# Log-sum-exp over 16,384 rows: the first load split into two 64-partition transfers on two queues

## The chip, the cores and the metric

The kernel runs on one core of a Trainium2 chip. The metric is device time in microseconds (us); three runs of the kernel before gave 161.6, 161.67 and 161.76, median 161.67.

The core has engines that run side by side and meet only at semaphores. ScalarE (ACT in the profile) computes exponentials and logarithms, VectorE (DVE) sums, GpSimd (POOL) adds, TensorE (PE) is used here for small checks alone, and SyncE (SP) issues transfers. Sixteen DMA engines move the data between the device's main memory and the on-chip memory, which has 128 partitions (rows).

## The reference

The input `x` is 32 x 512 x 1024 floats: 16,384 rows of 1,024, 67.1 MB. For each row the logarithm of the sum of exponentials is computed:

```python
max_x = np.max(x, axis=-1, keepdims=True)
return (max_x.squeeze(-1) + np.log(np.sum(np.exp(x - max_x), axis=-1))).astype(np.float32)
```

The output is 32 x 512 floats, 65.5 KB.

## The kernel before

**Work and tiles.** Each of the 128 partitions takes 128 rows. The kernel skips the maximum: it takes exponentials as they are, sums them, takes the logarithm, and checks on the side that no sum was too large or too small. Only if that check failed would a second, slower pass with the maximum run (lines 312 to 364); with this input it doesn't.

**The loads.** `LOADS` lists 18 loads by their size in rows per partition: 16, 16, 16, 16, 13.5, 12.5, 9, 7 and so on down to 0.47. A load is one transfer over all 128 partitions, issued on SP's queue by `load` (line 139); a load of 16 rows moves 16,384 floats, 64 KB, into each partition, 8.39 MB in all. Each load has a semaphore `landed[i]` that reaches 16 when all its data is there.

**The ring.** The loads go into `ring`, which has room for 48 rows per partition. Loads 0, 1 and 2 fill it. Load 3 takes the place of load 0 and must wait until the last reader of load 0 has finished; `users` keeps who that is, and `load` makes SP wait for it. So SP's queue is in order: a load that waits for its slots holds up those after it.

**The work on a load.** ACT waits for `landed[i]` and takes exponentials in place (line 228). Then the rows are summed in one of these ways, written behind each load's size in `LOADS`: R, one reduction on DVE (line 239); F, GpSimd adds the two halves of each row (line 233) and DVE reduces what is left (line 171); T, DVE adds the halves and sums in one instruction for each row (line 249); Y and Z, for the last row, ACT sums as it goes (line 202). Loads 0, 1 and 2 are all of kind R. At the end come two logarithms (lines 268, 281), two stores (lines 276, 285) and the check (lines 290 to 308).

**The first load.** A program opens with a barrier in which every engine drains its own queue and then waits for the others (line 407 in the profile, once more at line 62). ACT's first instruction behind it is the load of its function table (line 125). `start_early` takes the instruction of load 0 out of its place when the program is finished and puts it ahead of SP's first drain, so that load 0 is issued before that barrier. Loads 1 and 2 are issued by SP behind the barrier.

## Time and profile before

The profile is of one execution. Its times are in us from its first instruction; `ring<-in_x_dram` means that the ring is written from the input. The engines' busy shares and instruction counts:

| | busy us | share of the span | instructions |
|---|---|---|---|
| DVE | 114.3 | 71% | 59 |
| ACT | 114.5 | 71% | 31 |
| POOL | 37.3 | 23% | 11 |
| PE | 2.2 | 1% | 26 |

| | us |
|---|---|
| median of three runs | 161.67 |
| span of the profiled execution | 160.4 |
| around the span | 1.3 |

Issues of transfers are not counted as busy time; they appear in the timeline under SPq, where q stands for an engine's instruction queue. "mean" or a number of ns is for one instruction. A row in the timeline may merge several instructions (x2, x3): it has the first one's start and the time to the last one's end. In brackets stands how long the engine was idle before, and what ended that.

### The profile page before, as it was taken

The page shows a single profiled execution, that of the slowest core. Times are in us where ns is not written, and L with a number is a line of the kernel's source. Part 1 is how long each engine was busy: PE and PEld are TensorE (multiplying, and loading weights), DVE is VectorE, ACT ScalarE, POOL GpSimd, SP SyncE. Part 2 cuts the span into 40 slices and gives each one's busy share as a digit, 9 for nine tenths or more (in the row PEclk, how much of TensorE's full clock was granted, in tenths as well). Part 3 has the DMA queues.
Part 4 walks back from the last instruction along what each step waited for, and adds up shares of the span by engine and source line. Part 5 has one row for each costly group of instructions (what it writes and reads, how often), then busy time and mean ns, then how long its engine had stood idle before and what let it go on. Part 6 is the DMA issues. An engine that isn't in the chain of part 4 may idle for free.

```text
span 160.4 us, 219 instructions
## 1 busy us (share of the span) xinstructions
PE 2.2 (1%) x26; PEld 1.1 (1%) x26; DVE 114.3 (71%) x59; ACT 114.5 (71%) x31; POOL 37.3 (23%) x11
## 2 busy tenths in 40 slices
PE   0000000000000000000000000000000000000022
PEld 0000000000000000000000000000000000000011
DVE  0000000009999499994999859959999999999996
ACT  3000059990699708995099949991999989799996
POOL 0000000000000000000000994690004969891000
DMA  7996996996996996996999999999999999999992
GB/s 262 523 523 262 523 523 262 523 507 278 523 490 294 523 490 294 523 490 294 482 441 441 441 425 409 409 409 480 432 395 417 450 416 398 448 411 424 412 413 95
DMA packets 2881, 67.18 MB, mean 419 GB/s; under 512 B 576, under 2 KB 704, under 8 KB 1344
## 3 DMA queue, kind: packets, MB, share of 16 engines
q1 hardware_dynamic: 2880, 67.18, 97.7%
q14 instruction: 1, 0.01, 0.0%
HBM read 67.11 MB, written 0.07 MB: 419 GB/s over the span
## 4 chain that ended last, share of the span: by engine, by line
DMA 52%; ACT 28%; DVE 19%; issue 1%; PE 0%
DMA ring<-in_x_dram 52%; ACT ring L228 27%; DVE sumexp L239 15%; DVE sumexp L171 2%; DVE ring L249 1%; DVE over L301 0%; PE count L306 0%; ACT res L268 0%; DVE clamped L290 0%; DVE fine L308 0%; DVE sumexp L212 0%
## 5 line engine op out<-in xcount | busy, mean ns | idle before, releaser
L228 ACT ACTIVATE ring<-ring 128x16384 f32<-128x16384 f32 (+16 forms) x23 | 111.7, 4908 | 43.0 <-DMA ring<-in_x_dram 43.0
L239 DVE TENSOR_REDUCE sumexp<-ring 128x16 f32<-128x16384 f32 (+4 forms) x9 | 85.6, 9513 | 42.7 <-ACT ring L228 42.7
L233 POOL TENSOR_TENSOR ring<-ring 128x3072 f32<-128x3072 f32 (+3 forms) x7 | 37.1, 5313 | 107.3 <-ACT ring L228 107.3
L171 DVE TENSOR_REDUCE sumexp<-ring 128x6 f32<-128x3072 f32 (+3 forms) x7 | 18.4, 2656 | 0.0
L249 DVE SCALAR_TENSOR_TENSOR ring<-ring 128x512 f32<-128x512 f32 x15 | 9.6, 687 | 0.4 <-ACT ring L228 0.4
L125 ACT ACT_TABLE_LOAD x1 | 1.3, 1283 | 1.4 <-PEq L62 1.4
L156 PE MATMUL count<-far,bad 128*1 128x1 f32 x2 | 0.2, 164 | 153.2 <-DVE clamped L151 153.2
L160 PE MATMUL count<-sumexp,ones 128*1 128x1 f32 x18 | 1.6, 164 | 3.6 <-DVE ring L249 3.6
L249 DVE DVE_READ_ACCUMULATOR ring<-ring 128x1 f32 x15 | 1.2, 82 | 0.0
L202 ACT ACTIVATE last_exp<-ring 128x544 f32<-128x544 f32 (+1 forms) x2 | 1.2, 584 | 0.0
L126 DVE MEMSET ones<- 128x1 f32 x1 | 0.1, 59 | 1.5 <-PEq L62 1.5
L156 PEld LDWEIGHTS count<-far,bad 128*1 128x1 f32 x2 | 0.1, 80 | 153.2 <-DVE clamped L151 153.2
L160 PEld LDWEIGHTS count<-sumexp,ones 128*1 128x1 f32 x18 | 0.8, 80 | 4.5 <-DVE ring L249 4.5
L301 DVE SCALAR_TENSOR_TENSOR over<-ring 128x240 f32<-128x240 f32 x1 | 0.4, 404 | 0.0
L308 DVE TENSOR_SCALAR fine<-count 1x1 int32<-1x1 f32 x1 | 0.1, 147 | 0.3 <-PE count L306 0.3
L151 DVE SCALAR_TENSOR_TENSOR clamped<-clamped,sumexp 128x119 f32<-128x119 f32 x1 | 0.3, 283 | 0.0
L268 ACT ACTIVATE res<-sumexp 128x112 f32<-128x112 f32 x1 | 0.3, 279 | 0.0
L281 ACT ACTIVATE res<-last_sum,sumexp 128x1 f32<-128x1 f32 x1 | 0.3, 261 | 0.0
L202 ACT ACTIVATION_READ_ACCUMULATOR last_exp<-ring 128x1 f32 x2 | 0.3, 126 | 0.0
L146 DVE TENSOR_SCALAR clamped<-sumexp 128x119 f32<-128x119 f32 x1 | 0.2, 221 | 0.0
L279 ACT ACTIVATE res<-sumexp 128x15 f32<-128x15 f32 x1 | 0.2, 209 | 0.0
L290 DVE SCALAR_TENSOR_TENSOR clamped<-sumexp 128x9 f32<-128x9 f32 x1 | 0.2, 169 | 0.0
(17 smaller groups left out, 1.8 us busy)
## 6 DMA issues: line engine op xcount, KB each, us to landing
ring<-in_x_dram SPq DMA_DIRECT2D x1, 6912.0 KB, 23.9
ring<-in_x_dram SPq DMA_DIRECT2D x1, 6400.0 KB, 19.7
ring<-in_x_dram SPq DMA_DIRECT2D x1, 4608.0 KB, 15.9
ring<-in_x_dram SPq DMA_DIRECT2D x1, 3584.0 KB, 24.0
ring<-in_x_dram SPq DMA_DIRECT2D x1, 3072.0 KB, 19.1
ring<-in_x_dram SPq DMA_DIRECT2D x1, 2288.0 KB, 24.1
ring<-in_x_dram SPq DMA_DIRECT2D x1, 1664.0 KB, 20.9
ring<-in_x_dram SPq DMA_DIRECT2D x1, 1264.0 KB, 23.6
```

Of the source, the lines that this page charges most:

```text
L125: nc.scalar.preload_act_table_set("natural_log_exp_and_others")
L151: dve.did(nc.vector.scalar_tensor_tensor(out=clamped[:, 0:LATE], in0=clamped[:, 0:LATE], scalar=0.0, in1=sumexp[:, 0:LATE], op0=ALU.bypass ...
L156: pe.did(nc.tensor.matmul(count, lhsT=bad[:, 0:1], rhs=far, start=True, stop=False))
L160: return pe.did(nc.tensor.matmul(count, lhsT=ones, rhs=sumexp[:, c : c + 1], **kw))
L171: at = dve.did(nc.vector.reduce_sum(out=sumexp[:, c0 : c0 + s0], in_=halves, axis=AX.X))
L202: at = act.did(nc.scalar.activation(out=last_exp[:, here - p : end - p], in_=ring[:, here:end], func=AF.Exp, accum_out=first_sum if how == ...
L228: at = act.did(nc.scalar.activation(out=v, in_=v, func=AF.Exp))
L233: at = pool.did(nc.gpsimd.tensor_tensor(out=rows[:, :, 0:H], in0=rows[:, :, 0:H], in1=rows[:, :, H:d], op=ALU.add))
L239: who = (dve, dve.did(nc.vector.reduce_sum(out=sumexp[:, c : c + s], in_=rows, axis=AX.X)))
L249: who = (dve, dve.did(nc.vector.scalar_tensor_tensor(out=lo, in0=lo, scalar=1.0, in1=rows[:, r, H:d], op0=ALU.mult, op1=ALU.add, accum_out ...
L268: ln_early = act.did(nc.scalar.activation(out=res[:, 0:W], in_=sumexp[:, 0:W], func=AF.Ln))
L301: dve.did(nc.vector.scalar_tensor_tensor(out=over[:, 0:half], in0=last_piece[:, 0:half], scalar=CEILING, in1=last_piece[:, half : 2 * half ...
```

## The change

Load 0 is made as two transfers of 64 partitions: partitions 0 to 63 are issued by SP as before, partitions 64 to 127 by ACT, on ACT's own queue. Both add to `landed[0]`, so ACT waits there for 32 instead of 16. `start_early` now moves both instructions, each to a place ahead of the first drain of its own engine. All other loads stay single transfers of 128 partitions on SP's queue.

```diff
-        return nc.sync.dma_start(
-            out=ring[:, here : here + size], in_=source(done_before, size)
-        ).then_inc(landed[i], 16)
+        made = []
+        parts = [(nc.sync, 0, P // 2), (nc.scalar, P // 2, P)] if i == 0 else [(nc.sync, 0, P)]
+        for queue, p0, p1 in parts:
+            made.append(queue.dma_start(
+                out=ring[p0:p1, here : here + size], in_=source(done_before, size)[p0:p1]
+            ).then_inc(landed[i], 16))
+        return made
...
-        first_load = first_load or dma.ins
+        if i == 0:
+            first_loads.extend(one.ins for one in dma)
...
-        act.wait(landed[i], 16)
+        act.wait(landed[i], 16 * len(dma))
...
+        for load in first_loads:
+            here = next(b for b in blocks if any(i.name == load.name for i in b.instructions))
+            k = next(k for k, i in enumerate(here.instructions) if i.name == load.name)
+            assert not here.instructions[k].has_wait()
+            first = here.instructions.pop(k)
+            top = blocks[0].instructions
+            k = next(
+                k for k, i in enumerate(top)
+                if i.engine == first.engine and isinstance(i, mybir.InstDrain)
+            )
+            top.insert(k, first)
```

More of the change, by code (lines that the diff above doesn't have):

```diff
@@ L184 @@
     ln_early = None
-    first_load = None
+    first_loads = []
     for i, (size, ops) in enumerate(loads):
@@ L380, in start_early @@
         blocks = program.main_func.blocks
-        here = next(b for b in blocks if any(i.name == first_load.name for i in b.instructions))
-        k = next(k for k, i in enumerate(here.instructions) if i.name == first_load.name)
-        assert not here.instructions[k].has_wait()
-        first = here.instructions.pop(k)
-        top = blocks[0].instructions
-        k = next(
-            k for k, i in enumerate(top)
-            if i.engine == mybir.EngineType.SP and isinstance(i, mybir.InstDrain)
-        )
-        top.insert(k, first)
+        for load in first_loads:
[9 more added lines that the diff above has]
+            top.insert(k, first)
     nc.at_finalize(start_early)
```

## The prediction

> **What bounds the kernel now.** I read the page first: the sliced view, the queue table and the chain that ended last.

> ```profile
> span 160.4 us, 219 instructions
> ...
> DVE  0000000009999499994999859959999999999996
> ACT  3000059990699708995099949991999989799996
> ...
> DMA  7996996996996996996999999999999999999992
> GB/s 262 523 523 262 523 523 262 523 507 278 523 490 294 523 490 294 523 490 294 482 441 441 441 425 409 409 409 480 432 395 417 450 416 398 448 411 424 412 413 95
> ...
> q1 hardware_dynamic: 2880, 67.18, 97.7%
> ...
> DMA 52%; ACT 28%; DVE 19%; issue 1%; PE 0%
> ```

> The DMA row is full from the first slice to the last but one, and one hardware queue holds the 16 DMA engines for 97.7% of the span, while ACT and DVE have empty slices for the first third. (The 262/523 swing only means that rows of 64 KB are counted when they finish.) Then I asked for busy time by stretch, to see whether the engines have a hole anywhere.

> ```profile
> 0.00:10.00 10.00, 0.00 (x0) 0.00 (x0) 0.15 (x4) 1.28 (x1) 0.20 (x4) 1.00 1.03 419
> 10.00:20.00 10.00, 0.00 (x0) 0.00 (x0) 0.00 (x0) 0.00 (x0) 0.00 (x0) 1.00 0.97 419
> ...
> 60.00:80.00 20.00, 0.00 (x0) 0.00 (x0) 17.87 (x2) 13.86 (x1) 0.00 (x0) 1.00 1.01 437
> 80.00:100.00 20.00, 0.00 (x0) 0.00 (x0) 17.78 (x2) 17.59 (x3) 9.97 (x1) 1.00 1.00 433
> 100.00:120.00 20.00, 0.00 (x0) 0.00 (x0) 18.27 (x5) 16.68 (x4) 6.71 (x1) 1.00 0.95 411
> 120.00:140.00 20.00, 0.00 (x0) 0.00 (x0) 19.70 (x5) 18.43 (x6) 15.75 (x3) 1.00 1.00 431
> ```

> The last two columns are the DMA engines' busy share and GB/s. The only hole is 5% of 20 us, 1 us, between 100 and 120 us. So the transfer stream runs almost unbroken from the first load to the tail, and what lengthens one early load moves all that follows.

> The timeline gives the pace of that stream. A SPq row is the issue of a load; an ACT row in brackets with DMA as its releaser starts when a load has landed.

> ```profile
> 0.00 0.39 SPq L139 DMA_DIRECT2D ring<-in_x_dram  x1
> ```

> ```profile
> 1.45 0.84 SPq L139 DMA_DIRECT2D ring<-in_x_dram  x2
> ```

> ```profile
> 1.45 1.28 ACT L125 ACT_TABLE_LOAD   x1 [1.45 <-PEq L62]
> ...
> 22.00 13.86 ACT L228 ACTIVATE ring<-ring 128x16384 f32<-128x16384 f32 x1 [19.27 <-DMA ring<-in_x_dram]
> 35.89 17.22 DVE L239 TENSOR_REDUCE sumexp<-ring 128x16 f32<-128x16384 f32 x1 [34.23 <-ACT ring L228]
> 41.33 13.86 ACT L228 ACTIVATE ring<-ring 128x16384 f32<-128x16384 f32 x1 [5.46 <-DMA ring<-in_x_dram]
> 55.22 17.22 DVE L239 TENSOR_REDUCE sumexp<-ring 128x16 f32<-128x16384 f32 x1 [2.10 <-ACT ring L228]
> ```

> ```profile
> 60.68 13.86 ACT L228 ACTIVATE ring<-ring 128x16384 f32<-128x16384 f32 x1 [5.49 <-DMA ring<-in_x_dram]
> ...
> 80.02 13.95 ACT L228 ACTIVATE ring<-ring 128x9216 f32<-128x9216 f32 x2 [5.49 <-DMA ring<-in_x_dram]
> ```

> Loads 0 to 3 land at 22.00, 41.33, 60.68 and 80.02 us: 19.33 to 19.35 us for each 128 x 16384 floats, 8.39 MB, or 434 GB/s, 27.1 GB/s for each of 16 engines. That makes load 0's own transfer run from 22.00 - 19.33 = 2.67 us to 22.00 us. With 128 rows over 16 engines, 8 rows each, a row takes 19.33 / 8 = 2.42 us. The smaller loads keep this rate: 433 GB/s between 80 and 100 us with rows of 13.5 and 12.5 thousand floats.

> **The change, part by part.**

> *The issue.* SP's issue of load 0 becomes one for 64 rows, and ACT gains one. Price from the one that starts the timeline: 0.39 us for 128 rows, so 0.2 to 0.39 us on each engine. ACT stands idle at that point, as the rows of the opening barrier show:

> ```profile
> L407 ACTq DRAIN  x1: 8/8/8, 0.1 to 0.1; - x1
> ...
> L407 SPq DRAIN  x1: 133/133/133, 0.4 to 0.4; - x1
> L407 SPq EVENT_SEMAPHORE  x1: 17/17/17, 0.7 to 0.7; - x1
> L407 ACTq EVENT_SEMAPHORE  x1: 17/17/17, 0.7 to 0.7; - x1
> ```

> ACT reaches its drain at 0.1 us and then waits until 0.7. With an issue of up to 0.39 us and a drain that, like SP's, may then take 0.13, it arrives at 0.1 + 0.39 + 0.13 = 0.62 us, against 0.4 + 0.13 = 0.53 for SP now. The barrier moves by 0 to 0.1 us. Behind it on ACT stands the table load (1.45 to 2.73 us), not wanted before 22.00; on SP stand loads 1 and 2, issued at 1.45 and not wanted by the engines before load 0's rows are through at 22 us. The cover is 19 us in both cases, so the cost is nothing. Were the cover gone it would be 0.1 us. The wait of ACT's first exponential on 32 instead of 16 adds no instruction.

> *When the transfer starts.* It begins 2.67 us after its issue by the pace above. Shorter issues could bring that forward: by nothing at the least, by the whole 0.39 us at the most. I take 0, since the 2.28 us that are not issue stay.

> *What the transfer costs as two halves.* This is the term that decides. Each half is 4.19 MB on 64 partitions. If it is spread over all 16 engines, each has 4 rows of SP's half and 4 of ACT's: the same 8 rows, the same bytes. Every load and store of this trace is 128 partitions wide, so no row shows what a 64-partition transfer runs at; I bound it from both sides. Low end: 27.1 GB/s belongs to an engine, whatever partitions it writes. Then 8 rows take 8 x 2.42 = 19.33 us as before: a cost of 0. High end: 27.1 GB/s belongs to a place of entry into the on-chip memory that a fixed set of 8 partitions shares, which with 128 partitions in flight cannot be told from an engine. Sixteen engines that all work on the lower 64 partitions then press through half of the entries, and a row takes 4.84 us. Issued 0.1 us apart, both halves reach every engine in the same order, so the engines take a lower row together, then an upper row together: 8 x 4.84 = 38.7 us, a cost of 19.3 us. Below zero I see no more than the earlier start.

> The trace's nearest rows are the equal paces of loads with 16,384, 13,824 and 12,800 floats a row: a ceiling that doesn't move with the row's length, 16 times one number. A fixed set of 16 ways would give that, and these may sit at the engines or at the on-chip memory. I take the high end, as a judgement: 128 rows in 16 groups of 8 is a layout in which each engine has a way of its own, and 64 rows in 16 groups of 4 is not.

> [...]

> *How far the delay travels.* Load 0 lands at 22.0 + 19.3 = 41.3 us, load 1 behind it at 60.7. Load 3 overwrites load 0's slots and so is issued when DVE's first reduction ends, 35.89 + 17.22 = 53.11:

> ```profile
> 53.14 0.33 SPq L139 DMA_DIRECT2D ring<-in_x_dram  x1
> ```

> It moves to 72.5, while load 2 still occupies the engines to 80.0: the same 7.5 us in hand as now (60.68 - 53.14). Nothing catches up, because ACT and DVE work on a load only after it has landed and every later load sits behind the earlier ones in a stream with 1 us of holes; the chain through the later loads keeps its lengths:

> ```profile
> 55.22 17.23 DVE sumexp L239
> 72.45 0.02 issue
> 72.46 23.87 DMA ring<-in_x_dram
> ...
> 119.11 19.09 DMA ring<-in_x_dram
> 138.20 0.02 issue
> 138.22 12.34 ACT ring L228 x5
> ```

> *The sum.* The span is 160.4, and the median of the runs shown, 161.67, has 1.3 us around it. Issue 0, barrier 0, start 0, transfer +19.3: span 179.7, time 179.7 + 1.3 = 181.0 us. If engines that share an entry are a little out of step, each gains that lag on each row: 0.1 us of lag over 8 rows takes 0.8 us off, a lag of 0.3 us 2.4. The forecast's own range is therefore 178.5 to 181.7.

> **The rivals.**

> 1. *Nothing changes: the rate belongs to the engines.* For it: a DMA share of 0.97 to 1.03 at a rate that one number explains. Against it: nothing in this trace, which has no narrow transfer. The engines alternate between two queues, load 0 and load 1 land when they did, time 161.7 us. [...]

> 2. *The other side: it starts sooner.* The place is the 2.67 us before the first transfer, the price at most the issue's 0.39 us, and it decides only if the entries are no limit and load 0 is then on the path, which the full DMA row says it is. Time 161.67 - 0.39 = 161.3 us. Against it: 2.28 of the 2.67 us aren't issue.

> 3. *The engines fall out of step.* As in the forecast, but two engines that meet at an entry aren't served evenly; one gets ahead by a row, and from then on one writes the lower half while the other writes the upper. The loss is one to two rows, 2.42 to 4.84 us: about 165.3 us. For it: uneven starts would be enough. Against it: an even share preserves the lag that there was.

> 4. *The change doesn't do what it says: ACT's half doesn't run beside SP's but behind what SP has queued.* ACT's first exponential would then start when loads 1 and 2 are in too, at 60.68 instead of 22.00, load 3 would be issued at 60.68 + 13.86 + 17.22 = 91.8 instead of 53.14, and land some 22 us later at 113.8 instead of 80.02: +33.8, about 195 us. Against it: loads 1 and 2 are issued 1.3 us after ACT's half.

> **How the numbers follow.** Forecast 60%, unchanged 20%, sooner 9%, out of step 8%, behind 3%. The predicted time is the forecast's, 181.0. Leaving out the unchanged case would leave more than 2 in 10 outside, so the range reaches from the sooner case, 161.3, to 182.0; the likeliest case alone is 178.5 to 181.7. About 0.2%, 0.3 us, is what a measurement of this kernel can tell from no change: faster 0.09, same 0.20, slower 0.71 (forecast, out of step and behind).

> **What would show it.** In the changed profile ACT's first exponential should start near 41 us instead of 22, with the GB/s row at about 210 for the first ten slices and as before from then on, the DMA busy share still near 1 (the engines hold a row longer, they don't idle), and every later gap on ACT as it was. A first exponential near 22.0 us shows rival 1 and my choice of the high end wrong; one near 21.6, rival 2; near 24 to 27, rival 3; near 60, rival 4. A barrier that ends more than 0.2 us later than 1.45 would make the issue's price wrong. If load 0 lands late but the end moves by less than load 0 does, the one-for-one travel is wrong.

## The result, and the profile after

The changed kernel takes 181.66 us (median; 181.28 to 181.85) against 161.71 (161.6 to 161.79): a ratio of 1.123, 95% interval 1.1217 to 1.1244, 20 us slower. The forecast was 181.0.

From the page of the changed kernel, the sliced view and the queue table:

```profile
span 180.5 us, 220 instructions
...
DVE  0000000000005999699959997799699999999996
ACT  2000000005994399609990899499489998899996
...
DMA  9999999966999997999999999998999999999993
GB/s 232 232 232 232 232 232 218 218 203 290 465 465 465 436 421 334 436 465 465 465 436 421 429 392 392 502 420 386 455 408 408 432 457 398 435 420 425 421 408 104
...
q1 hardware_dynamic: 2816, 62.98, 86.9%
q10 hardware_dynamic: 80, 4.19, 10.8%
```

The DMA row is as full as before, so a reader of that row alone would see no trouble. The row below it shows it: 203 to 232 GB/s for the first nine slices of 4.5 us, about half the pace, then the old one. The engines are busy and slow, not idle. The second queue, q10, is ACT's, with the 4.19 MB of the upper half.

The timeline of the changed kernel, in start, duration, engine and line (its line 142 issues loads, 233 is the exponential, 244 the reduction):

```profile
0.12 0.55 ACTq L142 DMA_DIRECT2D ring<-in_x_dram  x1
...
2.13 1.28 ACT L125 ACT_TABLE_LOAD   x1 [2.13 <-PEq L62]
...
42.46 13.86 ACT L233 ACTIVATE ring<-ring 128x16384 f32<-128x16384 f32 x1 [39.05 <-DMA ring<-in_x_dram]
56.35 17.22 DVE L244 TENSOR_REDUCE sumexp<-ring 128x16 f32<-128x16384 f32 x1 [54.00 <-ACT ring L233]
61.43 13.86 ACT L233 ACTIVATE ring<-ring 128x16384 f32<-128x16384 f32 x1 [5.11 <-DMA ring<-in_x_dram]
```

The first exponential starts at 42.46 us instead of 22.00, the second at 61.43 instead of 41.33: 20.46 and 20.10 later. The chain that ended last, from the issue of load 4 to the tail, keeps the lengths it had, each piece some 20.1 us later (72.46, 119.11 and 138.22 before):

```profile
92.57 23.88 DMA ring<-in_x_dram
...
139.23 19.08 DMA ring<-in_x_dram
158.31 0.02 issue
158.33 12.35 ACT ring L233 x5
```

So the loss arises in load 0's transfer, and nothing behind load 1 takes any of it up. The trace also records every DMA packet by itself, here a row of 64 KB. By these records the last row of load 0 ended at 41.47 us instead of 21.64, 19.8 us later; the first exponential began 0.99 us behind it instead of 0.37. So 0.4 us of the delay of load 0's landing never reached what stands behind it.

### The profile page after: what moved, and what is told of

The parts are those of the page before. It is cut to its first block, busy times and chain, and to the rows that moved or that the text cites. A ratio compares the mean times of both kernels' runs of the same rounds, so it can differ in the third digit from the quotient of the medians.

```text
span 180.5 us, 220 instructions
## 1 busy us (share of the span) xinstructions
PE 2.2 (1%) x26; PEld 1.1 (1%) x26; DVE 114.2 (63%) x59; ACT 114.5 (63%) x31; POOL 37.4 (21%) x11
## 2 busy tenths in 40 slices
DMA packets 2897, 67.18 MB, mean 372 GB/s; under 512 B 592, under 2 KB 720, under 8 KB 1360
## 3 DMA queue, kind: packets, MB, share of 16 engines
q10 hardware_dynamic: 80, 4.19, 10.8%
## 4 chain that ended last, share of the span: by engine, by line
DMA 47%; ACT 32%; DVE 16%; another core or an unknown queue 3%; issue 1%; PE 0%
DMA ring<-in_x_dram 47%; ACT ring L233 32%; DVE sumexp L244 14%; DVE sumexp L175 2%; DVE ring L254 0%; DVE over L306 0%; PE count L311 0%; ACT res L273 0%; DVE clamped L295 0%; DVE fine L313 0%; DVE sumexp L217 0%
```

## The experiments

The same result has other possible causes: that the DMA engines lose pace when they alternate between two queues (Q below), or that a transfer's pace follows its number of partitions (N). P is the theory of the prediction, a supposition that no trace of before settles: that the limit sits where the rows land and the lower 64 partitions reach half of the ways in. Each edit below replaces the list of parts into which load 0 is made; the other loads are whole, as in the changed kernel (the last edit cuts load 6 instead). Where a range of columns stands in the list, the transfer moves those columns alone; otherwise all. A ratio is to the kernel before, run again beside the experiments: 161.66 us for the first three and the quarters, 161.76 for the others.

### Two queues, but all 128 partitions in each

```diff
-parts = [(nc.sync, 0, P // 2), (nc.scalar, P // 2, P)]
+parts = [(nc.sync, 0, P, 0, size // 2), (nc.scalar, 0, P, size // 2, size)]
```

> Load 0 is still two transfers, on SP's and ACT's queues ahead of the barrier, but split by columns: all 128 partitions in each, 8,192 floats a row. Theory P (the limit is where the rows land: 64 partitions on one side reach half of the entries): no cost, ACT's first exponential near 22.0 us, time 161.7 within 0.3. Theory Q (the 16 engines lose half their pace when they alternate between two queues): load 0 still takes 38.7 us, first exponential near 42, time 181 to 182. Theory N (the pace follows the number of partitions in a transfer): as P, 161.7.

Measured: 161.71 us, ratio 1.0001 (0.9992 to 1.0010). The timeline of this kernel:

```profile
0.12 0.37 ACTq L142 DMA_DIRECT2D ring<-in_x_dram  x1
1.58 1.28 ACT L125 ACT_TABLE_LOAD   x1 [1.58 <-PEq L62]
...
22.10 13.86 ACT L233 ACTIVATE ring<-ring 128x16384 f32<-128x16384 f32 x1 [19.25 <-DMA ring<-in_x_dram]
```

Two queues ahead of the barrier, and load 0 lands at 22.10. Q is out as a cause: alternating cost nothing that can be measured, 161.71 against 161.66 us. Nor did the concurrent issue from two queues win anything.

### Lower and upper half on one queue

```diff
+parts = [(nc.sync, 0, P // 2), (nc.sync, P // 2, P)]
```

> The two 64-partition halves, both issued by SP ahead of the barrier, ACT issues nothing there. P and N: each half takes 19.3 us by itself, one behind the other, first exponential near 41 to 42, time 181 to 182 as with two queues. Q: one queue, nothing to alternate with, time 161.7 and first exponential near 22.

Measured: 183.12 us, ratio 1.1326 (1.1309 to 1.1343). Busy time by stretch of this kernel, the last two columns being the DMA share and GB/s:

```profile
10.00:20.00 10.00, 0.00 (x0) 0.00 (x0) 0.00 (x0) 0.00 (x0) 0.00 (x0) 1.00 1.02 210
20.00:30.00 10.00, 0.00 (x0) 0.00 (x0) 0.00 (x0) 0.00 (x0) 0.00 (x0) 1.00 1.00 210
30.00:40.00 10.00, 0.00 (x0) 0.00 (x0) 0.00 (x0) 0.00 (x0) 0.00 (x0) 1.00 1.02 210
```

With a single queue the loss is there, even 1.5 us larger than on two. What cost the time is the cut into 64 partitions each, not who issues; whether their number or their place counts, this run doesn't say.

### Is it the number of partitions or which ones?

```diff
+parts = [(nc.sync, 32, 96), (nc.sync, 0, 32), (nc.sync, 96, P)]
```

> Load 0 as three transfers on SP's queue: partitions 32 to 95, then 0 to 31, then 96 to 127. P, with the entries laid out so that partitions 0 to 63 share one half of them and 64 to 127 the other: the first has half of its rows on either side and reaches all 16 entries, 4.19 MB in 9.7 us; the other two reach 8 each, 2.10 MB in 9.7 us each; in all 29.0 us instead of 19.3, first exponential near 31.7, time 171.4. N (pace in proportion to the number of partitions): 19.3 us for 64 and 19.3 us for each 32, 58 us, time 200. Q: 161.7.

Measured: 172.43 us, ratio 1.0663 (1.0647 to 1.0680). By stretch:

```profile
0.00:10.00 10.00, 0.00 (x0) 0.00 (x0) 0.15 (x4) 1.28 (x1) 0.20 (x4) 1.00 1.03 419
10.00:20.00 10.00, 0.00 (x0) 0.00 (x0) 0.00 (x0) 0.00 (x0) 0.00 (x0) 1.00 0.97 210
20.00:30.00 10.00, 0.00 (x0) 0.00 (x0) 0.00 (x0) 0.00 (x0) 0.00 (x0) 1.00 1.00 210
30.00:40.00 10.00, 0.00 (x0) 0.00 (x0) 0.00 (x0) 7.25 (x1) 0.00 (x0) 1.00 1.01 419
```

The three transfers can be read off: 64 partitions across the middle move at 419 GB/s, then the two of 32 at 210, then load 1 at 419. So the transfer of 64 partitions was not slow as such. And a transfer of 32 was not slower than a half of 64, 210 GB/s each, which N requires. N falls twice. The loss, 10.8 us, is half of the 21.5 of the one-queue halves, as half of the bytes moved at the half pace.

### Four transfers of 32, eight of 16

```diff
+parts = [(nc.sync, p, p + 32) for p in range(0, P, 32)]     # quarters
+parts = [(nc.sync, p, p + 16) for p in range(0, P, 16)]     # eighths
```

> Load 0 as four transfers of 32 partitions on SP's queue, 0-31, 32-63, 64-95, 96-127. P with that layout: 32 partitions reach as many entries as 64 of one side, 8, so each takes 9.7 us, in all 38.7, time 181 to 182 as with halves. N, or entries that belong to 8 neighbouring partitions: a quarter of the pace, 19.3 us each, 77.3 in all, time 220. Q: 161.7.

> Load 0 as eight transfers of 16 partitions on SP's queue. [...] Rival R (a transfer that stays on one side runs at half pace, however many partitions it has): 38.7 us in all, time 181 to 183, as with halves and quarters.

Measured: quarters 182.74 us, ratio 1.1303 (1.1285 to 1.1320); eighths 216.28 us, ratio 1.3353 (1.3324 to 1.3382). The first fence is a stretch of the quarters, the second two of the eighths:

```profile
20.00:30.00 10.00, 0.00 (x0) 0.00 (x0) 0.00 (x0) 0.00 (x0) 0.00 (x0) 1.00 1.00 210
```

```profile
20.00:40.00 20.00, 0.00 (x0) 0.00 (x0) 0.00 (x0) 0.00 (x0) 0.00 (x0) 1.00 0.93 105
40.00:60.00 20.00, 0.00 (x0) 0.00 (x0) 0.00 (x0) 0.00 (x0) 0.00 (x0) 1.00 0.93 105
```

```profile
76.62 13.86 ACT L233 ACTIVATE ring<-ring 128x16384 f32<-128x16384 f32 x1 [70.52 <-DMA ring<-in_x_dram]
```

That is 54.6 us later than 22.00, or 73.9 us for load 0 instead of 19.3, 9.24 for each eighth. So R, that staying on one side simply halves the pace, falls: 113 GB/s for 16 partitions of one side against 206 for 32. A fixed number of ways in that partitions share would fit these paces; that there are such, and which partitions would share one, no run shows. The straddling transfer bore out the two sides alone. Four times 2.42 us a row would have given 161.7 + 58 = 220 us; the eighths came out 3.7 us below that, since a row took 9.25 us; why, stays open.

### The same change, with the partitions dealt out even and odd

```diff
-parts = [(nc.sync, 0, P // 2), (nc.scalar, P // 2, P)]
+parts = [(nc.sync, 0, 2), (nc.scalar, 1, 2)]      # ring[p0:P:step]
```

> Load 0 as two transfers of 64 partitions on SP's and ACT's queues: the even partitions and the odd ones. [...] S (what counts is that a transfer has rows on both sides, or how many entries it reaches in all): no cost, time 161.7. [...]

Measured: 161.99 us, ratio 1.0018 (1.0008 to 1.0028). This is the closest relative of the change: two transfers of 64 partitions, on the same two queues, with the same bytes and the same issues, as its timeline shows, and all but 0.3 us of the loss is gone.

```profile
0.12 0.55 ACTq L142 DMA_DIRECT2D ring<-in_x_dram  x1
2.13 1.28 ACT L125 ACT_TABLE_LOAD   x1 [2.13 <-PEq L62]
...
22.58 13.86 ACT L233 ACTIVATE ring<-ring 128x16384 f32<-128x16384 f32 x1 [19.16 <-DMA ring<-in_x_dram]
```

Its queue table has ACT's half hold the engines for 6.0% of a span of 160.8 us, against 10.8% of 180.5 in the changed kernel. For the four rows of that half on each engine, that is 2.4 us a row against 4.9.

```profile
q10 hardware_dynamic: 80, 4.19, 6.0%
```

S held. A half pace here, 181 to 182 us, I had expected as well, on a guess of which rows are taken at the same time that no run shows; it did not come. What the runs say is that the transfers with half of their partitions on either side of 64 moved at the full pace: 419 GB/s for partitions 32 to 95, and 419 in the first 20 us for the even and the odd 64.

One thing stays tied in all runs: a partition always reads its own part of the main memory, so where a row lands is never separated from where it is read. Partitions 32 to 95 read 64 rows at the same distances from each other as 0 to 63 do, and at twice the pace (419 against 210 GB/s), which speaks against a limit in how the rows lie in the main memory. That there are ways in, and that they are those of the on-chip memory, is argued from that, not shown.

### The same cut in a later load

```diff
-parts = [...] if i == 0 else [(nc.sync, 0, P)]
+parts = [(nc.sync, 0, P // 2), (nc.sync, P // 2, P)] if i == 6 else [(nc.sync, 0, P)]
```

> Load 0 whole and early as before; load 6 (9 rows a partition, 4.72 MB, 10.9 us at the full pace) as a lower and an upper half on SP's queue. P: 4.72 MB at 205 to 216 GB/s take 21.8 to 23.0 us, 10.9 to 12.1 more, and the transfer stream is the bound there too: time 172.6 to 173.8. Rival F (the loss comes with the start of a program, when queues and engines begin): 161.7. If the stretch from 100 us on has room to take part of it up: between 162 and 172.

Measured: 173.77 us, ratio 1.0746 (1.0728 to 1.0764), 12.0 us slower, at the upper end of what was expected. From the timeline:

```profile
134.48 7.98 ACT L233 ACTIVATE ring<-ring 128x5120 f32<-128x5120 f32 x2 [11.72 <-DMA ring<-in_x_dram]
138.98 5.49 DVE L244 TENSOR_REDUCE sumexp<-ring 128x5 f32<-128x5120 f32 x1 [12.44 <-ACT ring L233]
```

ACT, which had waited half a microsecond for load 7 and none for load 6 at this stage, now stands 11.72 us for load 6. The loss has nothing to do with the start of the program: it follows the bytes moved at the half pace. The one-queue halves lost 21.5 us on 16 rows a partition, which makes 12.1 for nine, so the hole between 100 and 120 us takes none of it up.

## Why the prediction was right

**What bounds the kernel.** Right: the transfer stream. An early load that landed 20.5 us later moved the end by 20.1, and a middle one (load 6), whose half-pace rows were to cost 10.9 to 12.1, moved it by 12.0. By the sign that I had named, the end moving by less than load 0, the one-for-one travel fails by 0.4 us; that part lies behind load 0's last row and never reached the stream.

**The transfer as two halves.** The high end was the right choice: a row took 4.87 us against the 4.84 expected. At the time it was a judgement between 0 and 19.3 us that no row of the trace could settle, and the range from 161.3 to 182.0 held "nothing changes" as well; so wide a range says little, the sum of 181.0 and the signs say more. The runs have shown that the pace hung on which partitions a transfer took: the even and odd transfers differ from the halves only in which partitions go together (2.4 us a row against 4.9), and the straddling one has the halves' size at the full pace (419 GB/s against 210). That the limit lies at ways into the on-chip memory stays argued, as said above. The term was put at 19.3 and measured 20.1 in the span. The deduction for engines a little out of step, 0.8 to 2.4 us, did not show; the deviation went the other way. The engines were in fact further apart than the 0.1 to 0.3 us assumed: by the packet records their first rows ended between 5.51 and 7.35 us, and each further row of load 0 still took 4.82 to 4.97 us. Which engines, if any, shared a way, the records don't say.

**The issue.** Wrong in size. I bounded an issue of 64 rows by 0.39 us, that of 128 rows; it took 0.55 on both engines, and both then drain longer. The first row is of SP, the fence behind it of the barrier:

```profile
0.00 0.55 SPq L142 DMA_DIRECT2D ring<-in_x_dram  x1
```

```profile
L413 SPq DRAIN  x1: 367/367/367, 0.6 to 0.6; - x1
L413 ACTq DRAIN  x1: 529/529/529, 0.7 to 0.7; - x1
L413 SPq EVENT_SEMAPHORE  x1: 17/17/17, 1.4 to 1.4; - x1
```

The barrier so ended at 2.13 instead of 1.45 us, 0.68 later against the "0 to 0.1" predicted and beyond the 0.2 that I had named as a refutation. That the later barrier costs nothing was right: the even and odd kernel has the same issues and the same barrier at 2.13, and the table load still ends 19 us before it is wanted.

**When the transfer starts.** I took 0, between nothing and 0.39 us earlier. The even and odd kernel, where the pace is full, shows load 0 landing at 22.58 instead of 22.00 and the span 0.4 us longer (160.8 against 160.4): later, not sooner, a side that I had not allowed for. The 2.67 us were a wrong reading, too: in the packet records the first row of load 0 starts at 1.02 us in the kernel before. I had counted every row at 2.42 us, but the first ones took up to 3.56, and the exponential began 0.37 us behind the last one. In the changed and in the even and odd kernel the first row starts at 1.34 us. Of the 0.8 us by which the span outgrew the sum (20.1 against 19.3), this later start accounts for 0.3; eight rows at 4.87 instead of 2.42 us take 19.6 us more, not 19.3, which is another 0.3; the last 0.2 I have not taken apart. In all nine kernels the start goes with the length of the first issue: the first row starts at 1.01 to 1.04 us where that issue took 0.38 to 0.39, at 1.33 to 1.40 where it took 0.55 to 0.61. That the longer issue is what delays the start fits this, but no run changes the issue alone.

**The rivals.** "Nothing changes" fell with the first exponential at 42.46, "sooner" with it; "out of step" expected 24 to 27 and "behind" about 60.

## What to carry to other kernels

Before a transfer is cut, ask which partitions each part writes. Cut along the columns, load 0 cost nothing here (161.71 us), nor did it with each part having as many partitions below 64 as from 64 on: every second one took 161.99 us in all, and 32 to 95 moved at the full 419 GB/s. Cut at 64, its lower and upper half took twice the time of the whole, 40.1 us from the first row's start to the last one's end against 20.6. A second queue added no pace where the 16 DMA engines were already full (161.71 against 161.66 us). And read the GB/s row beside the busy row: here the engines were as busy at half the pace as at the full one (a DMA share of 1.00 at 216 GB/s between 10 and 30 us, 0.97 at 419 before).

## What was unexpected of the hardware

The issue of each 64-partition transfer took longer than that of 128: 0.55 us against 0.39, with the drain behind it on SP 0.37 against 0.13 us, in the changed kernel and in the even and odd one alike, while the two 128-partition issues of half the columns took 0.39 and 0.37. Fewer partitions alone didn't make it longer: the first issue of the quarters and that of the eighths took 0.39 us as well.

The lower and upper half on one queue were slower than on two, 183.12 against 181.66 us. The packet records show where: a row took 5.1 us on average instead of 4.87, 0.2 us more for each of eight rows. Why a row took longer when both halves came from one queue is open.
